# The bonus sums of an RWKV-7 block as narrow float32 strips, with their stores, spreading load and product re-queued

## The chip, the cores and the metric

The kernel runs on one core of one Trainium2 chip. The metric is the device time of one execution in microseconds. Three runs of the kernel before gave 989.61, 990.5 and 990.91; the median is 990.5.

## The reference

One layer of a hybrid trunk for 512 tokens of width 2048, with 16 learned tokens put ahead. One input projection feeds two groups: RWKV-7 time mixing with 16 heads of 64 channels, and a gated short convolution. The part that matters here is the time mixing's bonus term, with r, k and v of shape (tokens, heads, 64):

```python
rh = r.reshape(bsz, L, H, N)
kh = k.reshape(bsz, L, H, N)
vh = v.reshape(bsz, L, H, N)
...
bonus = jnp.sum(rh * kh * r_k[l], axis=-1, keepdims=True) * vh
y_a = (yn + bonus.reshape(bsz, L, D_RWKV)) * jax.nn.silu(g_r)
```

For every token and head the 64 products r k r_k are summed, and the sum scales that head's 64 values of v. Beside it stands the squared length of every k, which normalises the keys (`kk`), the recurrence over tokens, the convolution, the output projection and two norms over the width. Everything is float32; the output is (1, 512, 2048).

## The kernel before

Channels lie on the partitions, tokens run along the rows of a tile, and two heads of 64 channels make one tile of 128: eight head pairs, i = 0 to 7. The projections are products of 128 x 128 weights with 256 or 512 tokens. Weights come from HBM as float32 (tile wr, 128 x 1024), ACT casts each half to a rounded high part and DVE subtracts it from the raw half for a low part (L151, L152, "w"); three products (high with high, low with high, high with low) keep float32 accuracy (L353, L368).

`mains()` is a generator that issues the projections in a fixed order (the lists ps_k, ps_r, ps_v, ps_g, then ps_C, ps_h, ps_B, ps_gc of the convolution) and brings the weights ahead. The other work is laid between them: `fill(ns)` runs the generator for so many nanoseconds of PE work by the planner's own count, `until("v", i)` runs it until that tile is ready, and `later(ns, f)` puts a function, mostly one DMA, into a list that runs when the planner's clock has gone so far; each of these is put behind the newest weight load (`state["dma"]`). So the order on every queue is written by these numbers, and each engine and each DMA queue then takes its instructions in that order. All DMAs of this part are issued by SP.

`prepare(i)` does the time mixing's work for a pair that doesn't depend on the recurrence. It makes the decay and the factors of the chunks (ar, bk), multiplies r by k and r_k in place (L735), forms the Gram products of the chunks on PE (L755, tiles g, and L766 for the 16 learned tokens), and sums the squares of k over each head: `key_norms` (L786) takes the 576 columns of sq in four strips of 144, each a product with a 32-column matrix of ones and zeros at its own 32 columns of PE (L788). For the bonus it splits r into a high and a low part (rk_h by ACT, rk_l by DVE, L665 and L666), multiplies each with a 128 x 128 matrix of ones (two blocks of 64) into zb (L820, L821), which leaves every channel of a head with that head's sum, copies zb over r (L822), multiplies r by v when v is ready (L919) and has it stored to HBM 12500 ns later (rbd, L920). It is loaded again for the last stage (L1227).

Masked Gram blocks go to HBM (sg) and come back as 16 x 16 diagonal blocks (d); the norms take the same way (sn, nd). DVE inverts the blocks step by step into y (L862 to L888). y goes to HBM (sx, L903) and comes back as xT and xo (`load_inverse`, L894 and L895); SP issues these by `later` too, in odd pairs 20500 and 22500 ns on (pair 1: 22500 and 24500). After every odd pair `invert` takes two pairs together: it turns xT into xn by DVE (L948), and PE forms t from it and the Gram blocks (L963). `next_banks` and the pools give the PSUM tiles; "ser" and "misc" are two of their tags.

Other names below: bd, vd, opd, gated and mixd are tensors in HBM to which SP stores; ex is a small product of DVE with which the projection of a shifted tile begins (L403), u, hh and cv are tiles of the convolution, gc and g are gates.

Of the kernel before, what the change touches and what calls it, by code (L numbers as in the profile page):

```python
# [9 lines left out]
F32 = mybir.dt.float32  # L10
F32R = mybir.dt.float32r
I32 = mybir.dt.int32
AF = mybir.ActivationFunctionType
ALU = mybir.AluOpType
# [4 lines left out]
P = 128  # L19
DM = 2048  # L20
KT = DM // P
SEQ = 512
META = 16
L = SEQ + META
CH = 64
NCH = SEQ // CH + 1
LP = NCH * CH
# [5 lines left out]
C_ID, C_GM, C_BM, C_ON = 0, 128, 384, 512  # L33
# [11 lines left out]
    tr=3200, lev=3000, cp=4200, out=1500, begin=19500, p=2900, u=2900, s=4200, mid=1000, last=3700, mix=2600,  # L45
# [44 lines left out]
def hymba_kernel(ctx: ExitStack, tc: tile.TileContext, xt, xtok, front, w_in, w_out, pv, lup, cst, msk, gf, out):  # L90
    nc = tc.nc
    ctx.enter_context(tc.manual_schedule(engines={mybir.EngineType.PE}))
    cp = ctx.enter_context(tc.tile_pool(name="cp", bufs=1))
    dp = ctx.enter_context(tc.tile_pool(name="dp", bufs=2, space=DRAM))
# [3 lines left out]
    cs = cp.tile([P, C_N], F32, name="cs")  # L98
# [74 lines left out]
    rst = xp.tile([P, 4], F32, name="rst")  # L173
    rsx = cq.tile([P, 2 * META], F32, name="rsx")
    la = cq.tile([P, 2, L], F32R, name="la")
    ones = xp.tile([P, P], F32R, name="ones")
    omm = xp.tile([P, 33], F32, name="omm")
    hv = xp.tile([P, 6, 8], F32, name="hv")
    hl = cp.tile([P, 2, 8], F32, name="hl")
# [9 lines left out]
    def tr(name, dt=F32):  # L189
        return cq.tile([P, LP], dt, tag="tr", name=name, bufs=5)  # L190
# [134 lines left out]
            out=hv[:, 4], in0=pvt[:, V_KA : V_KA + 8], scalar1=-0.5, scalar2=1.0, op0=ALU.mult, op1=ALU.add  # L325
        )

    nc.scalar.copy(ones, cs[:, C_BM : C_BM + P])
    FULL = ((0, 272), (272, L))
    TAIL = ((14, 272), (272, L))  # L330
    REAL = ((META, L),)
# [264 lines left out]
    def later(ns, fn):  # L596
        pending.append((clock[0] + ns, fn))
        pending.sort(key=lambda e: e[0])
# [16 lines left out]
    def fill(ns):  # L615
        while ns > 0:
            seen = len(ready)
            t = step()
            if t is None:
                return  # L620
            ns -= t
            if len(ready) > seen:
                ns += FW["evac"]
# [35 lines left out]
        nc.vector.tensor_tensor(out=lo, in0=raw, in1=hi.bitcast(F32), op=ALU.subtract)  # L659
        return hi, lo  # L660

    def split(t, name, n):
        hi = tr(f"{name}_h", F32R)[:, 0:n]
        lo = tr(f"{name}_l", F32R)[:, 0:n]
        nc.scalar.copy(hi, t)  # L665
        nc.vector.tensor_tensor(out=lo, in0=t, in1=hi.bitcast(F32), op=ALU.subtract)  # L666
        return hi, lo

    heads = [(h, slice(64 * h, 64 * h + 64), slice(64 - 64 * h, 128 - 64 * h)) for h in range(2)]

    place = [(i % 2) * 4 + i // 2 for i in range(NPAIR)]
# [11 lines left out]
    def behind(dst, src):  # L683
        with tc.issue_after(state["dma"]):
            nc.sync.dma_start(dst, src)
# [8 lines left out]
    def prepare(i):  # L694
# [43 lines left out]

        sq = tr(f"sq{i}")
        nc.scalar.activation(sq, k, AF.Square, scale=col(V_KK, i))  # L740
        rh, rl = split(r, f"rk{i}", SEQ)
        fill(FW["gram_b" if p else "gram"] + FW["meta"].get(i, 0))

        late = state["step"] > 48
# [16 lines left out]

        def gram_meta():
            z = early or next_banks()
            norms = key_norms(z[0][:, 96 : 96 + NS]) if late else None
            for h, hs, ho in heads:
                nc.tensor.matmul(  # L766
                    z[h][:, 0:META],
                    bk[hs, 0, h : h + 2, :].rearrange("p a s -> p (a s)"),
                    ar[hs, 0, 0, 0:META],
                    start=True, stop=True,  # L770
                )
            norms = norms if late else key_norms(z[0][:, 96 : 96 + NS])
            if p and "levels" in state:
                state["out"] = state.pop("levels").pop(0)(second_level(z))
            with ahead():
                for h in range(2):
                    nc.vector.tensor_tensor(
                        out=gt[:, h, 0, 0:META], in0=z[h][:, 0:META], in1=gmask[:, h, 0:META], op=ALU.mult
                    )
            with ahead():  # L780
                nc.scalar.copy(n2, norms)
            if "out" in state:
                state.pop("out")()
            state["banks"] = z

        def key_norms(z):  # L786
            for j in range(4):
                nc.tensor.matmul(  # L788
                    z[32 * j : 32 * j + 32], cs[:, C_BM + 48 : C_BM + 80], sq[:, j * NS : (j + 1) * NS],
                    start=True, stop=True, tile_position=(0, 32 * j),  # L790
                )
            return z
# [11 lines left out]

        NS = LP // 4
        n2 = tr(f"n2{i}")[:, 0:NS]
        if late:
            gram_meta()
        za = [pz.tile([P, 4, P], F32, tag="tz", name=f"g{i}_1_{h}") for h in range(2)]
# [4 lines left out]
            gram_meta()  # L814
        masked(za, 1, 5)
        masked(zc, 5, 9)
        fill(FW["gram2"] - FW["meta"].get(i, 0))

        zb = pi.tile([P, SEQ], F32, tag="ser", name=f"zb{i}")
        nc.tensor.matmul(zb, ones[:, 0:P], rh, start=True, stop=False)  # L820
        nc.tensor.matmul(zb, ones[:, 0:P], rl, start=False, stop=True)  # L821
        nc.scalar.copy(r, zb)  # L822
        fill(FW["misc"])


        bt = cq.tile([P, 2, NCH - 1, CH], F32, tag="bt", name=f"bt{i}")
        for a in range(2):
# [9 lines left out]
        def blocks(t):  # L837
            return bass.AP(tensor=t.tensor, offset=t.offset, ap=[[BLK, 8 * NCH], [CH, 16], [1, 16]])
# [9 lines left out]
            stash_later(5500 + 1000 * h, i, gt[ho, h], O_KK, 2 * CH, 64 * h, 64)  # L848
            stash_later(7500 + 1000 * h, i, gt[hs, h, :, CH:P], O_BR, CH, 64 * h, 64)
        nd = cq.tile([NB, 16], F32, tag="nd", name=f"nd{i}")  # L850
        behind(d, blocks(sg))
        behind(nd, sn.rearrange("(p s) -> p s", s=16))
        y = cq.tile([NB, 256], F32, tag="y", name=f"y{i}").rearrange("p (s t) -> p s t", t=16)
        nc.gpsimd.memset(y, 0.0)
        nc.vector.tensor_scalar(out=nd, in0=nd, scalar1=1e-24, scalar2=None, op0=ALU.max)
# [60 lines left out]
                    ))  # L916
        until("v", i)
        v = got["v", i]
        nc.vector.tensor_tensor(out=r, in0=r, in1=v[:, CH:LP], op=ALU.mult)  # L919
        later(12500, lambda: nc.sync.dma_start(rbd[i], r))  # L920
        fill(FW["v"])

        vs = cq.tile([P, NCH, CH], F32, tag="vs", name=f"vs{i}")
# [769 lines left out]
```

## Time and profile before

| what | value |
|---|---|
| runs | 990.5 us median (989.61 to 990.91) |
| profiled execution | 989.51 us, its span 987.6 |
| PE | 978.7 us busy, granted clock 0.998 |
| DVE, ACT, POOL | 707.0, 390.4, 127.6 us busy |
| DMA | 176.89 MB, mean 179 GB/s |

A row of the timeline has the start and the length in us, the engine, the line in the kernel, the operation, what it writes and reads, the shapes, and how many instructions the row holds; in brackets stands the idle time ahead and who ended it. PEld is the loading of weights into PE, which runs beside the products. SPq rows are the time in which SP issues a DMA, not the transfer.

### The profile page before, as it was taken

The numbers are of one execution on the slowest core, as the hardware profiler recorded it, in microseconds if no ns is written. First come the engines' busy times: TensorE is split into PE (matmuls) and PEld (weight loads), VectorE is DVE, ScalarE is ACT, GpSimd is POOL, SyncE is SP. The second block draws the span as 40 slices with busy tenths as digits, with TensorE's granted clock in tenths as the row PEclk, the third lists the DMA queues.
The fourth block names the chain that finished last, engine by engine and source line by source line (L and its number), as shares of the span: only waits on it lengthen the run. The fifth ranks groups of instructions, "written<-read, shape, count | busy, mean of one in ns | idle before, by whom it ended". The sixth has DMA issues, their size and how long they took to land.

```text
span 987.6 us, 23392 instructions
## 1 busy us (share of the span) xinstructions
PE 978.7 (99%) x9511; PEld 907.1 (92%) x9511; DVE 707.0 (72%) x1415; ACT 390.4 (40%) x730; POOL 127.6 (13%) x241
## 2 busy tenths in 40 slices
PE   9999999999999999999999999999999999999996
PEld 9999999999998999998999998989889898888885
DVE  6787966578675779653778754355756698997896
ACT  7653432344312434322434323222332326556464
POOL 0120202112010121010111010011211102001001
PEclk9999999999999999999999999999999999999999
DMA  9526586246675374853275856999784798797654
GB/s 323 161 90 159 136 209 168 76 130 146 154 184 166 91 194 116 210 152 112 85 184 123 205 143 188 272 249 270 217 266 118 220 278 221 190 320 182 157 128 170
DMA packets 205532, 176.89 MB, mean 179 GB/s; under 512 B 138545, under 2 KB 168049, under 8 KB 205041
## 3 DMA queue, kind: packets, MB, share of 16 engines
q1 hardware_dynamic: 202976, 166.76, 60.9%
q0 software_dynamic: 2304, 8.39, 5.0%
q8 instruction: 74, 1.21, 0.5%
q14 instruction: 34, 0.27, 0.1%
q10 hardware_dynamic: 144, 0.26, 0.1%
HBM read 139.02 MB, written 36.35 MB: 178 GB/s over the span
## 4 chain that ended last, share of the span: by engine, by line
PE 96%; DVE 2%; issue 1%; DMA 0%; ACT 0%; POOL 0%; POOLq 0%; DVEq 0%; ACTq 0%
PE ps_v L353 9%; PE ps_h L353 9%; PE ps_C L353 9%; PE ps_g L353 9%; PE ps_B L368 9%; PE ps_gc L368 9%; PE ps_k L353 8%; PE ps_r L353 8%; PE M L1384 7%; PE P L1384 3%; PE Q L1384 2%; PE g L755 2%; PE ps_k L368 1%; PE ps_r L368 1%; PE ps_lora L368 1%; PE zy L1141 1%
## 5 line engine op out<-in xcount | busy, mean ns | idle before, releaser
L151 ACT CAST w<-wr 128x512 fp32r<-128x512 f32 x252 | 153.7, 619 | 294.1 <-PE ps_C L353 46.0
L152 DVE TENSOR_TENSOR w<-wr,w 128x512 fp32r<-128x512 f32 x252 | 174.1, 703 | 121.4 <-ACT w L151 120.2
L353 PE MATMUL ps_v<-xh,w 128*128 128x256 f32 (+2 forms) x512 | 84.0, 284 | 0.0
L368 PE MATMUL ps_B<-xh,w 128*128 128x512 f32 x256 | 83.4, 394 | 0.0
L353 PE MATMUL ps_h<-xh,w 128*128 128x256 f32 (+2 forms) x512 | 81.7, 281 | 0.0
L353 PE MATMUL ps_g<-xh,w 128*128 128x256 f32 (+2 forms) x512 | 81.4, 281 | 0.0
L368 PE MATMUL ps_gc<-xh,w 128*128 128x512 f32 x256 | 81.2, 392 | 0.0
L353 PE MATMUL ps_C<-xh,w 128*128 128x256 f32 (+2 forms) x512 | 80.8, 280 | 0.0
L353 PEld LDWEIGHTS ps_v<-xh,w 128*128 128x128 f32 x512 | 73.9, 188 | 0.3
L353 PE MATMUL ps_k<-xh,w 128*128 128x256 f32 (+1 forms) x448 | 73.3, 285 | 0.0
L353 PE MATMUL ps_r<-xh,w 128*128 128x256 f32 (+1 forms) x448 | 72.6, 281 | 0.0
L353 PEld LDWEIGHTS ps_g<-xh,w 128*128 128x128 f32 x512 | 72.0, 189 | 0.6 <-issue 0.2
L353 PEld LDWEIGHTS ps_h<-xh,w 128*128 128x128 f32 x512 | 72.1, 189 | 0.3
L353 PEld LDWEIGHTS ps_C<-xh,w 128*128 128x128 f32 x512 | 71.7, 189 | 0.2
L353 PEld LDWEIGHTS ps_k<-xh,w 128*128 128x128 f32 x448 | 64.7, 188 | 0.4
L353 PEld LDWEIGHTS ps_r<-xh,w 128*128 128x128 f32 x448 | 63.5, 189 | 0.4 <-issue 0.2
L353 PE MATMUL ps_h<-xl,w 128*128 128x256 f32 x256 | 57.3, 281 | 0.0
L368 PEld LDWEIGHTS ps_gc<-xh,w 128*128 128x128 f32 x256 | 47.8, 188 | 10.0
L368 PEld LDWEIGHTS ps_B<-xh,w 128*128 128x128 f32 x256 | 47.9, 188 | 9.6
L353 PE MATMUL ps_C<-xl,w 128*128 128x256 f32 x256 | 56.2, 280 | 0.0
L353 PE MATMUL ps_v<-xl,w 128*128 128x256 f32 x256 | 55.8, 278 | 0.0
L353 PE MATMUL ps_g<-xl,w 128*128 128x256 f32 x256 | 55.4, 278 | 0.0
(383 smaller groups left out, 2141.2 us busy)
## 6 DMA issues: line engine op xcount, KB each, us to landing
wr<-in_w_in_dram SPq DMA_DIRECT2D x126, 512.0 KB
ct<-opd SPq DMA_DIRECT2D x72, 192.0 KB
wo<-in_w_out_dram SPq DMA_DIRECT2D x24, 512.0 KB
x<-in_w_out_dram POOLq DMA_DIRECT2D x16, 512.0 KB, 6.0
opd<-ar SPq DMA_DIRECT2D x8, 576.0 KB
opd<-gt SPq DMA_DIRECT2D x16, 288.0 KB
bd<-bt SPq DMA_DIRECT2D x64, 64.0 KB
bw<-bd SPq DMA_DIRECT2D x16, 256.0 KB
```

The costliest lines, as they stand in the source:

```text
L151: nc.scalar.copy(hi, rq)
L152: low[q] = eng.tensor_tensor(out=lo, in0=rq, in1=hi.bitcast(F32), op=ALU.subtract).ins
L353: nc.tensor.matmul(ps[r][:, 0 : b - a], ww[:, k * P : (k + 1) * P], xx[:, kt, a:b], start=(kt == 0 and n == 0), stop=(kt == KT - 1 and n = ...
L368: nc.tensor.matmul(ps[r], ww[:, w], xx[:, kt, a:b], start=(kt == 0 and n == 0), stop=(kt == KT - 1 and n == 2))
L755: nc.tensor.matmul(z[h][:, c - c0], bk[hs, c, h : h + 2, :].rearrange("p a s -> p (a s)"), ar[hs, c].rearrange("p a s -> p (a s)"), start= ...
L1141: nc.tensor.matmul(zy[e][hs if e else ho, k], t[hs, o : o + CH], x, start=(n == 0), stop=(n == 2))
L1384: nc.tensor.matmul(bank[s], left(prod, jj, m, s), w, start=(jj == 0 and n == 0), stop=(jj == 7 and n == 2))
```

## The change

The high and low part of r, the two products with the matrix of ones, the copy of zb and the matrix itself go. r is float32 when it reaches PE: four strips of 128 of its 512 columns follow the four strips of the key norms, into the other bank of the same pair. ACT copies the 128 x 128 result (nb). Four of its rows hold one head's sums, for 128 tokens each, and four others the other head's; they are stored to HBM (sb) by two small DMAs, one for each head, put behind the load of the diagonal blocks d, and one DMA that reads each head's 512 sums 64 times spreads them over r again (256 KB, 4800 ns on the planner's clock). The load d itself is now issued behind the newest weight load without the helper. r x v is no longer issued when v is ready: it waits on the planner's clock, 18000 ns in odd pairs, 12500 in even ones, 10500 in pair 0, and is put behind the newest low part of a weight. Its store follows 3000 ns later.

```diff
-        rh, rl = split(r, f"rk{i}", SEQ)
...
-            norms = key_norms(z[0][:, 96 : 96 + NS]) if late else None
+            if late:
+                norms, bonus = sums_of(z)
...
             with ahead():
                 nc.scalar.copy(n2, norms)
+                nc.scalar.copy(nb, bonus)
...
-        def key_norms(z):
+        def sums_of(z):
+            return head_sums(z[0][:, 96 : 96 + NS], sq, NS), head_sums(z[1][:, 96 : 96 + P], r, P)
+
+        def head_sums(z, x, n):
             for j in range(4):
                 nc.tensor.matmul(
-                    z[32 * j : 32 * j + 32], cs[:, C_BM + 48 : C_BM + 80], sq[:, j * NS : (j + 1) * NS],
+                    z[32 * j : 32 * j + 32], cs[:, C_BM + 48 : C_BM + 80], x[:, j * n : (j + 1) * n],
                     start=True, stop=True, tile_position=(0, 32 * j),
                 )
...
-        fill(FW["gram2"] - FW["meta"].get(i, 0))
-
-        zb = pi.tile([P, SEQ], F32, tag="ser", name=f"zb{i}")
-        nc.tensor.matmul(zb, ones[:, 0:P], rh, start=True, stop=False)
-        nc.tensor.matmul(zb, ones[:, 0:P], rl, start=False, stop=True)
-        nc.scalar.copy(r, zb)
-        fill(FW["misc"])
-
+        fill(FW["gram2"] - FW["meta"].get(i, 0) + FW["misc"])
...
-        behind(d, blocks(sg))
+        with tc.issue_after(state["dma"]):
+            asked = nc.sync.dma_start(d, blocks(sg)).ins
         behind(nd, sn.rearrange("(p s) -> p s", s=16))
+        sb = dp.tile([2 * SEQ], F32, tag="sb", name=f"sb{i}")
+
+        def put_sums():
+            with tc.issue_after(asked):
+                for h in range(2):
+                    nc.sync.dma_start(sb[h * SEQ : (h + 1) * SEQ].rearrange("(j s) -> j s", s=P), nb[16 * h : P : 32])
+
+        spread = bass.AP(tensor=sb.tensor, offset=sb.offset, ap=[[SEQ, 2], [0, CH], [1, SEQ]])
+        later(1000, put_sums)
+        later(4800, lambda: nc.sync.dma_start(r, spread))
...
-        nc.vector.tensor_tensor(out=r, in0=r, in1=v[:, CH:LP], op=ALU.mult)
-        later(12500, lambda: nc.sync.dma_start(rbd[i], r))
+
+        def bonus_rows():
+            assert ("v", i + 1) not in ready
+            with tc.issue_after(low[max(low)]):
+                nc.vector.tensor_tensor(out=r, in0=r, in1=v[:, CH:LP], op=ALU.mult)
+
+        wait = 18000 if p else 12500 if i else 10500
+        later(wait, bonus_rows)
+        later(wait + 3000, lambda: nc.sync.dma_start(rbd[i], r))
```

The lines behind the change lie 2 to 8 further on or back: the turning of xT is L948 before and L956 now, the loads xT L894 and L895, sx L903 and L904, vd L927 and L935, r x v L919 and L924, rbd L920 and L928, the strips L788 and L784.

What moved is seen at three places. First SP in pair 1, around the inverse's way through HBM (sx, xT and xo belong to it, wr are weights), before:

```order
L159 DMA wr_2149<-in_w_in_dram 128x1024
L927 DMA vd<-vs_1938 32x9x32 x2
L159 DMA wr_2172<-in_w_in_dram 128x1024
L927 DMA vd<-vs_1938 32x9x32
L903 DMA sx_135<-y_1869 72x16x16
L927 DMA vd<-vs_1938 32x9x32
L159 DMA wr_2229<-in_w_in_dram 128x1024
L894 DMA xT_1906<-sx_135 64x9x64
L895 DMA xo_1907<-sx_135 64x4x64
L894 DMA xT_1906<-sx_135 64x9x64
```

Now:

```order
L935 DMA vd<-vs_1937 32x9x32
L928 DMA rbd_79<-r_1309 128x512
L935 DMA vd<-vs_1937 32x9x32
L159 DMA wr_2174<-in_w_in_dram 128x1024
L935 DMA vd<-vs_1937 32x9x32
L904 DMA sx_134<-y_1867 72x16x16
L935 DMA vd<-vs_1937 32x9x32
L159 DMA wr_2231<-in_w_in_dram 128x1024
L895 DMA xT_1904<-sx_134 64x9x64
L896 DMA xo_1905<-sx_134 64x4x64
L895 DMA xT_1904<-sx_134 64x9x64
```

Before, rbd stood further up, ahead of the last four bd stores and of all vd stores; now it stands between two vd stores, ahead of sx and of the loads xT.

Second, DVE in pair 3 where it takes the projection ps_C (ex). tt, y and prod are steps of the inverse, xn is the even pair's. Before:

```order
L152 TENSOR_TENSOR w_3752<-wr_3747,w_3752 128x512
L862 TENSOR_TENSOR tt_3674<-d_3665,nd_3666 72x8
L863 TENSOR_TENSOR y_3669<-tt_3674,nd_3666 72x8
L873 TENSOR_TENSOR prod_3673<-d_3665,y_3669 72x8
L948 STREAM_TRANSPOSE xn_4065<-xT_3080 128x512
L879 TENSOR_REDUCE tt_3674<-prod_3673 72x4
L882 TENSOR_TENSOR prod_3673<-y_3669,tt_3674 72x8
L152 TENSOR_TENSOR w_3781<-wr_3779,w_3781 128x512
L888 TENSOR_REDUCE y_3669<-prod_3673 72x2x2
L403 TENSOR_TENSOR ex<-ps_C_1_3513,rst 128x4
L873 TENSOR_TENSOR prod_3673<-d_3665,y_3669 72x8
```

Now:

```order
L152 TENSOR_TENSOR w_3756<-wr_3751,w_3756 128x512
L401 TENSOR_TENSOR ex<-ps_C_1_3512,rst 128x4
L863 TENSOR_TENSOR tt_3674<-d_3664,nd_3665 72x8
L864 TENSOR_TENSOR y_3669<-tt_3674,nd_3665 72x8
L874 TENSOR_TENSOR prod_3673<-d_3664,y_3669 72x8
L956 STREAM_TRANSPOSE xn_4070<-xT_3079 128x512
L880 TENSOR_REDUCE tt_3674<-prod_3673 72x4
L883 TENSOR_TENSOR prod_3673<-y_3669,tt_3674 72x8
L889 TENSOR_REDUCE y_3669<-prod_3673 72x2x2
L874 TENSOR_TENSOR prod_3673<-d_3664,y_3669 72x8
```

ex has moved ahead of the first steps of the inverse, of xn and of a low part, which follows it now (it stands further down).

Third, the end of the same stretch on DVE, and SP beside it. DVE before, from the second half of hh to the odd pair's xn:

```order
L404 TENSOR_TENSOR hh_4007<-ps_h_1_3885,rs 128x256
L490 SCALAR_TENSOR_TENSOR cv_4014<-u_3870,pvt,cv_4014 128x512 x2
L152 TENSOR_TENSOR w_3878<-wr_3876,w_3878 128x512
L152 TENSOR_TENSOR w_3881<-wr_3876,w_3881 128x512
L152 TENSOR_TENSOR w_3915<-wr_3913,w_3915 128x512
L152 TENSOR_TENSOR w_3918<-wr_3913,w_3918 128x512
L948 STREAM_TRANSPOSE xn_4066<-xT_3706 128x512
```

Now:

```order
L402 TENSOR_TENSOR hh_4013<-ps_h_1_3889,rs 128x256
L488 SCALAR_TENSOR_TENSOR cv_4020<-u_3874,pvt,cv_4020 128x512 x2
L152 TENSOR_TENSOR w_3882<-wr_3880,w_3882 128x512
L152 TENSOR_TENSOR w_3885<-wr_3880,w_3885 128x512
L152 TENSOR_TENSOR w_3919<-wr_3917,w_3919 128x512
L152 TENSOR_TENSOR w_3922<-wr_3917,w_3922 128x512
L924 TENSOR_TENSOR r_3151<-r_3151,v_3326 128x512
L956 STREAM_TRANSPOSE xn_4071<-xT_3706 128x512
```

The product of r and v stands behind four low parts, directly ahead of xn. SP before:

```order
L473 DMA gated_89<-g_3734 128x512
L927 DMA vd<-vs_3729 32x9x32 x4
L903 DMA sx_135<-y_3669 72x16x16
L927 DMA vd<-vs_3729 32x9x32 x2
L894 DMA xT_3706<-sx_135 64x9x64
L895 DMA xo_3707<-sx_135 64x4x64
L894 DMA xT_3706<-sx_135 64x9x64
L895 DMA xo_3707<-sx_135 64x4x64
```

Now:

```order
L935 DMA vd<-vs_3730 32x9x32 x4
L904 DMA sx_134<-y_3669 72x16x16
L928 DMA rbd_81<-r_3151 128x512
L935 DMA vd<-vs_3730 32x9x32 x2
L895 DMA xT_3706<-sx_134 64x9x64
L896 DMA xo_3707<-sx_134 64x4x64
L895 DMA xT_3706<-sx_134 64x9x64
L896 DMA xo_3707<-sx_134 64x4x64
```

The store rbd stands between sx and the loads xT; before, it stood further up, behind the fourth of eight bd stores.

More of the change, by code (lines that the diff above doesn't have):

```diff
@@ L175, in hymba_kernel @@
     la = cq.tile([P, 2, L], F32R, name="la")
-    ones = xp.tile([P, P], F32R, name="ones")
     omm = xp.tile([P, 33], F32, name="omm")
@@ L326, in hymba_kernel @@
         )
-    nc.scalar.copy(ones, cs[:, C_BM : C_BM + P])
     FULL = ((0, 272), (272, L))
@@ L660, in lora_up @@
         return hi, lo
[L662 to L667, printed above, removed]
     heads = [(h, slice(64 * h, 64 * h + 64), slice(64 - 64 * h, 128 - 64 * h)) for h in range(2)]
@@ L771, in gram_meta @@
                 )
-            norms = norms if late else key_norms(z[0][:, 96 : 96 + NS])
+            if not late:
+                norms, bonus = sums_of(z)
             if p and "levels" in state:
@@ L806, in prepare @@
         n2 = tr(f"n2{i}")[:, 0:NS]
+        nb = tr(f"nb{i}")[:, 0:P]
         if late:
```

## The prediction

> **What bounds the kernel now.** I read the page first, then the chain of waits, then the timeline of single engines at the places that the change touches.
>
> ```profile
> span 987.6 us, 23392 instructions
> PE 978.7 (99%) x9511; PEld 907.1 (92%) x9511; DVE 707.0 (72%) x1415; ACT 390.4 (40%) x730; POOL 127.6 (13%) x241
> PE 96%; DVE 2%; issue 1%; DMA 0%; ACT 0%; POOL 0%; POOLq 0%; DVEq 0%; ACTq 0%
> ```
>
> PE is busy for 99% of the span and is 96% of the chain that ended last. So the time moves by two things only: PE work taken out, and PE waits put in. Work on ACT, DVE or a queue counts only where it makes PE wait. The sum is made against the profiled execution, 989.51 us (987.6 of span, 1.9 outside it); the median of the runs is 990.5, so 1.0 is added at the end. A difference of 0.2%, 2.0 us, is about what can be told from none.
>
> **The PE work.** This is PE at head pair 0 (start, length, engine, line, operation; x8 means eight records in the row):
>
> ```profile
> 83.26 0.45 PE L788 MATMUL ps_v<-sq,cs 128*32 128x144 f32 x8
> 83.64 1.23 PE L353 MATMUL ps_r<-xh,w 128*128 128x260 f32 x8
> 87.50 0.40 PE L820 MATMUL zb<-rk_h,ones 128*128 128x512 f32 x1
> 87.97 0.28 PE L353 MATMUL ps_r<-xl,w 128*128 128x256 f32 x1
> ```
>
> The two removed products (L820, and L821 right behind it) take 87.97 - 87.50 = 0.47 us. What comes in are four float32 strips 32 columns of PE wide, over 128 columns, of the form that the key norms have over 144: those are eight records (two passes of four strips), and the next product starts 83.64 - 83.26 = 0.38 later. So the strips run side by side. The new four stand directly behind them, in the same form; scaled by columns they take 0.38 x 128/144 = 0.34 at most, and since part of the 0.38 is the change of form, which is paid once anyhow, at least about half, 0.19. I take 0.27: a gain of 0.20 a pair, 1.6 in eight (between 8 x 0.13 = 1.0 and 8 x 0.28 = 2.2).
>
> [...]
>
> ```profile
> L735 DVE SCALAR_TENSOR_TENSOR r<-r,hv,ta x8: 701/726/747, 75.1 to 528.1; 128x512 f32<-128x512 f32 x8
> L919 DVE TENSOR_TENSOR r<-r,v x8: 680/690/693, 89.0 to 546.7; 128x512 f32<-128x512 f32 x8
> L920 SPq DMA_DIRECT2D rbd<-r x8: 439/480/488, 97.5 to 557.7; - x8
> ```
>
> These are all instructions of a line (least, median, greatest ns; first and last start). The sums need r (L735), done at 75.1 + 0.7 in pair 0, far ahead of the norms at 83.26, so PE doesn't wait there. ACT loses a cast and a copy, DVE a low part, for one 128x128 copy; PE covers both engines (40% and 72% busy), so this counts nothing.
>
> **What the change moves.** The product r x v (L919, 0.69 on DVE) now stands behind late low parts, and the store rbd (L920, 0.48 on SP) waits for it. SP takes its requests in order. In the new order rbd stands ahead of the loads xT of the odd pairs (and in pair 1 ahead of the store sx that they read), and the turning of xT (L948) is what PE needs next for t (L963). Before:
>
> ```profile
> 155.31 0.37 SPq L903 DMA_DIRECT2D sx<-y  x1
> 151.92 0.93 SPq L927 DMA_DIRECT2D vd<-vs  x2
> 162.23 0.61 SPq L894 DMA_DIRECT2D xT<-sx  x1
> 158.04 2.38 DVE L152 TENSOR_TENSOR w<-wr,w 128x512 fp32r<-128x512 f32 x2
> 162.26 0.69 DVE L414 TENSOR_TENSOR gc<-ps_gc,rs 128x512 f32<-128x512 f32 x1 [1.85 <-PE ps_gc L368]
> 169.36 0.70 DVE L948 STREAM_TRANSPOSE xn<-xT 128x512 f32<-128x512 f32 x1
> 169.43 1.36 PE L963 MATMUL t<-xn,gt 64*64 64x32 f32 x64
> ```
>
> Pair 1: the product now stands between the two low parts that end at 158.04 + 2.38 = 160.42 and gc. It is done by 161.1, within DVE's idle 1.85. But SP, which had sent sx at 155.31, now holds at rbd until 161.1: rbd, a vd, a wr and a vd, four issues of about 0.45 (two vd take 0.93), put sx at 162.9. How long a transfer takes is seen at pair 3:
>
> ```profile
> 287.26 0.30 SPq L903 DMA_DIRECT2D sx<-y  x1
> 291.35 0.31 POOL L854 MEMSET y<- 72x256 f32 x1 [1.45 <-DMA sx<-y]
> 291.31 0.60 SPq L894 DMA_DIRECT2D xT<-sx  x1
> 292.64 0.61 SPq L894 DMA_DIRECT2D xT<-sx  x1
> 295.96 0.71 DVE L948 STREAM_TRANSPOSE xn<-xT 128x512 f32<-128x512 f32 x1 [1.32 <-DMA xT<-sx]
> 298.00 1.14 PE L963 MATMUL t<-xn,gt 64*64 64x32 f32 x64
> ```
>
> POOL and SP are both released at 291.3, so sx takes 4.05 from its issue; the second xT, 1.33 behind the first, takes 295.96 - 292.64 = 3.3. Hence in pair 1: 162.9 + 4.05 = 167.0, second xT issued at 168.3, there at 171.6, turned at 172.3. PE wants it half way through t, at about 170.1 (the first half uses the even pair). The wait is 2.2; in pair 5 (below) sx was through in 2.8, and with 2.8 for both transfers 0.4 of the wait is left; with 0.8 more of issue it is 3.0. I take 1.8.
>
> [...]
>
> Pair 3 has two losses in a row. These are DVE, POOL and PE there:
>
> ```profile
> 272.51 0.16 DVE L862 TENSOR_TENSOR tt<-d,nd 72x8 f32<-72x8 f32 x1
> 274.62 0.69 DVE L152 TENSOR_TENSOR w<-wr,w 128x512 fp32r<-128x512 f32 x1 [0.69 <-ACT w L151]
> 275.23 0.15 DVE L888 TENSOR_REDUCE y<-prod 72x4 f32<-72x8 f32 x1
> 276.72 0.16 DVE L403 TENSOR_TENSOR ex<-ps_C,rst 128x4 f32<-128x4 f32 x1 [1.34 <-PE ps_C L353]
> 286.51 0.68 DVE L888 TENSOR_REDUCE y<-prod 72x64 f32<-72x512 f32 x1
> 288.04 0.41 DVE L404 TENSOR_TENSOR hh<-ps_h,rs 128x256 f32<-128x256 f32 x1
> 288.60 1.30 POOL L485 TENSOR_TENSOR u<-u,hh 128x514 f32<-128x514 f32 x1
> 290.69 1.54 DVE L490 SCALAR_TENSOR_TENSOR cv<-u,pvt,cv 128x512 f32<-128x512 f32 x2 [2.24 <-ACT cv L487]
> 292.14 2.49 DVE L152 TENSOR_TENSOR w<-wr,w 128x512 fp32r<-128x512 f32 x4
> 292.93 0.61 PE L368 MATMUL ps_B<-xh,w 128*128 128x512 f32 x2
> ```
>
> DVE waits for PE at ex (276.72). Before, six small steps of the inverse's y, the turning of the even pair's xT and one low part run ahead of it, from 272.51 to 275.38; in the new order they stand behind ex. Without the idle 0.69 they take 2.2, and from ex to the last step of y DVE has no idle time. The two last steps of y now stand between the halves of hh, which lets one half (0.35 of DVE's time) go ahead of them. So y ends at 287.2 + 2.2 + 0.35 = 289.75, and hh, two short instructions later, at 290.3 instead of 288.45. Through u and cv this 1.85 reaches the first low part, which ended at 292.14 + 0.69 = 292.83 and now ends at 294.7; PE uses it in the second product of the row at 292.93, at 293.15. That is a wait of 1.5. (The distances from ex hold whatever PE lost or gained earlier.) The four low parts then end at 296.5, r x v behind them at 297.2, and only then does SP send rbd, 0.48, two vd, 0.93, and the xT loads: the first at 298.6, the second at 300.0, there at 303.3, turned at 304.0. PE would have wanted it at 298.57, half of the 1.14 from 298.00. In all 5.4 of waiting, the 1.5 among them. With 2.8 for xT it is 4.9; if the delay behind ex does not come about, r x v ends at 295.3 and 3.5 is left; with two half microseconds of issue more it is 6.5. I take the middle, 5.0.
>
> Pairs 5 and 7 have the same queue, but more room:
>
> ```profile
> 421.04 0.30 SPq L903 DMA_DIRECT2D sx<-y  x1
> 423.80 0.60 SPq L894 DMA_DIRECT2D xT<-sx  x1
> 426.40 0.75 DVE L432 SCALAR_TENSOR_TENSOR g<-pr_g,omm,sh_g 128x512 f32<-128x512 f32 x1
> 433.80 1.14 PE L963 MATMUL t<-xn,gt 64*64 64x32 f32 x64
> ```
>
> r x v follows g there, at 427.1 to 427.8. There SP sends sx ahead of rbd, and it is through in 423.80 - 421.04 = 2.8, so nothing waits for sx. rbd, vd, wr and vd take 1.8; the xT loads now go out at 429.6 and 430.9, the second is there at 434.2 and turned at 434.9, against a need at 434.4. That is 0.5 in pair 5 and, in the same pattern 147 us later, 0.5 in pair 7; nothing or 1.5 each at the ends. I take 0.8 for both.
>
> In the even pairs SP also holds at rbd, longest in pair 2. Behind it stand weights and vd stores:
>
> ```profile
> 232.69 0.44 SPq L159 DMA_DIRECT2D wr<-in_w_in_dram  x1
> 245.62 0.68 DVE L152 TENSOR_TENSOR w<-wr,w 128x512 fp32r<-128x512 f32 x1
> 259.28 0.28 PE L353 MATMUL ps_g<-xl,w 128*128 128x256 f32 x1
> ```
>
> In pair 2 the product follows the low part at 245.62, so rbd goes at about 247 and the weights sent at 232.69 at 248. With 5 us of transfer (an estimate, one more than sx's 4.05) and 1.3 for cast and low part they are ready at 254.3; by the order of the instructions PE's first use of their low part is the product at 259.28. Five microseconds of cover are left, so this counts nothing. If the cover were gone in all four even pairs by 1 us each, it would be 4.
>
> The sum: -1.6 + 1.8 + 5.0 + 0.8 = +6.0, 995.5 in the profiled execution and **996.5** against the median.
>
> **The rivals.** *Covers hold.* r x v and the transfers behind it come early enough that PE never waits: behind a held SP few requests are open, and sx and xT land faster than in any row above. For it: DVE is busy only 72% and loses a low part a pair; against it: SP's order is fixed, and at pair 3 PE's first use is only 293.15 - 292.83 = 0.32 behind the low part. Then only the PE work counts, -1.6: 988.9, down to 988.3 at the end of its bounds, with no wait in pair 3 as the point that decides; not slower. Chance 0.25.
>
> *Pair 3 alone.* One wait of 1.5 to 3.5 comes and the others are covered: -1.6 + 1.5 to 3.5 = -0.1 to +1.9, 991.5. For it: nowhere else is the room so small; against it: the hold of SP is the same in pair 1. Chance 0.16.
>
> *The strips run one after another.* Eight passes of 128 columns at a quarter of the 0.23 of a product over 512 are 0.47, what was removed: no gain, and 998 with the waits. Against it stands the row of the norms, eight records in 0.38. Chance 0.04. *Weights late too:* the four microseconds of the even pairs on top, 1000.5. For it speaks the long hold of SP, against it the cover of 5. Chance 0.09.
>
> The forecast keeps 0.46, with 993 to 1000 as its own range.
>
> **How the numbers follow.** Slower by over 0.2% (above 992.5) are the forecast, the last two rivals and a little of the second: 0.46 + 0.13 + 0.03 = 0.62. Within 0.2% are most of the second rival and nearly half of the first, 0.13 + 0.11 = 0.24; faster by over 0.2%, under 988.5, is left with 0.14, the end at which the strips cost least and nothing waits. The range from 988.8 to 1000.5 leaves out about two in ten.
>
> **What would show it.** Right: L784 in eight records more in about 0.25 us, a PE wait of 4 to 6 us between 290 and 306 at the products ps_B and t, released by DVE w and xn; xn waiting for the DMA xT at pair 1 and 3; rbd on SP released by DVE r. Wrong: no PE wait of over 1 us in the list of waits, or xT loads that land as early as before; then r x v or the transfers were not where I put them. PE waits at low parts in the even pairs would show the third case.

## The result and the profile after

The changed kernel takes 1016.51 us (median; 1014.11 to 1018.24), beside 990.7 of the kernel before on the same chip: a ratio of 1.0256, interval 1.0241 to 1.0271. It is slower, as forecast, but by 25.8 us and not by 6.0, and 1016.5 lies outside the range. The profiled execution took 1015.02, with a span of 1013.0; against the profiled 989.51 that is 25.5 more.

These lines of the page of the changed kernel are the busy time of the engines, the granted clock in 40 slices and the chain that ended last:

```profile
PE 987.9 (98%) x9559; PEld 915.5 (90%) x9559; DVE 703.9 (69%) x1407; ACT 382.9 (38%) x721; POOL 133.2 (13%) x241
PEclk9999998999899999999999999999999999999999
PE 82%; DVE 9%; DMA 4%; issue 2%; SPq 1%; ACT 1%; POOL 1%; POOLq 0%; DVEq 0%; ACTq 0%
```

Two things are to be seen. PE has fallen from 96% to 82% of the chain: PE waits now. And PE is busy for 9.2 us more than before (978.7), although the change takes PE work out; with that goes a clock that drops to 8 tenths in two slices. The waits of PE, from the list of waits of the same kernel (total, times, longest):

```profile
PE t L971 <- DVE xn L956: 12.9, 4, 4.0
PE ps_C L757 <- DVE pr_g L402: 3.0, 1, 3.0
```

How late PE is can be read at one group, the products z behind t (instructions, durations, first and last start). First the kernel before, then the changed one:

```profile
L976 PE MATMUL z<-xT,ts x128: 219/219/240, 174.1 to 586.4; 64*64 64x32 f32 x128
```

```profile
L984 PE MATMUL z<-xT,ts x128: 219/219/240, 179.7 to 611.7; 64*64 64x32 f32 x128
```

At pair 1 they start 5.6 us late, at pair 7 25.3: all that was lost was lost by then. The same comparison for each of the 6096 projection products, which have the same order in both kernels, gives the steps below. A stop is the distance of two successive starts on PE less what is usual for that product; a step is what PE's lateness grew by from just ahead of the stop until the lateness is level again.

| where | stop of PE | step of its lateness | step less stop |
|---|---|---|---|
| pair 1, t | 3.84 | 6.1 | 2.3 |
| pair 2, Gram product L757 | 3.25 | 6.1 | 2.9 |
| pair 3, ps_B and t | 0.78 + 4.23 | 6.7 | 1.7 |
| pair 5, t | 3.72 | 5.2 | 1.5 |
| pair 7, t | 1.94 | 3.5 | 1.5 |
| sum | 17.8 | 27.6 | 9.9 |

Beside the steps the lateness falls by 0.1 to 0.3 at every pair's strips, 2.0 in all: 27.6 - 2.0 = 25.6. The last column is the surprise. Here is what lies behind it at pair 1, in windows of 1 us (the window, its length, busy time and instructions of PE, PEld, DVE, ACT and POOL, then the granted clock, the share of the DMA engines and GB/s):

```profile
170.00:171.00 1.00, 0.00 (x0) 0.00 (x0) 0.94 (x2) 0.14 (x1) 0.00 (x0) 1.00 0.45 103
172.00:173.00 1.00, 0.00 (x0) 0.00 (x0) 0.71 (x1) 0.00 (x0) 0.00 (x0) 0.52 0.62 102
175.00:176.00 1.00, 1.00 (x6) 1.00 (x5) 0.00 (x0) 0.00 (x0) 0.00 (x0) 0.50 1.02 412
178.00:179.00 1.00, 1.00 (x8) 1.00 (x7) 0.53 (x1) 0.00 (x0) 0.00 (x0) 0.57 0.14 48
```

PE stands still in the first two rows. Towards the end of the stop the granted clock falls to half, and it stays there until 178.9, for 5.9 us after PE has its data at 173.0. Half of these, 2.9, is somewhat more than what PE loses beside the wait (2.3). Behind the other four places the clock is at half for 6.8 us (pair 2) and for 3.4 us each (pairs 3, 5 and 7).

The strips did what they were to do (PE at pair 0, as in the prediction's first row on the PE work):

```profile
83.21 0.45 PE L784 MATMUL ps_v<-sq,cs 128*32 128x144 f32 x8
83.48 0.40 PE L784 MATMUL ps_v<-r,cs 128*32 128x128 f32 x8
83.81 1.23 PE L351 MATMUL ps_r<-xh,w 128*128 128x260 f32 x8
```

From the first strip of the norms to ps_r it is 83.81 - 83.21 = 0.60 where it was 83.64 - 83.26 = 0.38: the four new strips cost 0.22, against 0.47 for what was removed. Eight times 0.25 are the 2.0 above.

**The places.** Pair 1, SP and then DVE:

```profile
160.57 0.34 SPq L928 DMA_DIRECT2D rbd<-r  x1
162.50 0.37 SPq L904 DMA_DIRECT2D sx<-y  x1
167.11 0.62 SPq L895 DMA_DIRECT2D xT<-sx  x1
169.35 0.61 SPq L895 DMA_DIRECT2D xT<-sx  x1
172.28 0.71 DVE L956 STREAM_TRANSPOSE xn<-xT 128x512 f32<-128x512 f32 x1 [1.34 <-DMA xT<-sx]
```

Pair 2, in the order SP, DVE, ACT, PE; this wait was not forecast:

```profile
252.18 0.70 DVE L924 TENSOR_TENSOR r<-r,v 128x512 f32<-128x512 f32 x1
252.90 0.34 SPq L928 DMA_DIRECT2D rbd<-r  x1
253.81 0.45 SPq L159 DMA_DIRECT2D wr<-in_w_in_dram  x1
258.99 1.14 ACT L151 CAST w<-wr 128x512 fp32r<-128x512 f32 x2 [5.89 <-DMA wr<-in_w_in_dram]
259.64 1.29 DVE L152 TENSOR_TENSOR w<-wr,w 128x512 fp32r<-128x512 f32 x2 [4.40 <-ACT w L151]
260.85 0.42 DVE L402 TENSOR_TENSOR pr_g<-ps_g,rs 128x256 f32<-128x256 f32 x1
261.32 0.60 PE L757 MATMUL ps_C<-ar,bk 64*128 64x16 f32 x2 [3.02 <-DVE pr_g L402]
```

The weights behind rbd land 5.2 us after their issue, so the low parts are late. What PE waits for is not these low parts. It is pr_g, the emptying of the bank that the Gram product L757 writes next, and it stands behind the low parts in DVE's order.

Pair 3, SP, DVE and PE:

```profile
308.02 0.34 SPq L928 DMA_DIRECT2D rbd<-r  x1
310.81 0.61 SPq L895 DMA_DIRECT2D xT<-sx  x1
313.86 0.71 DVE L956 STREAM_TRANSPOSE xn<-xT 128x512 f32<-128x512 f32 x1 [5.87 <-DMA xT<-sx]
305.63 0.73 PE L366 MATMUL ps_B<-xh,w 128*128 128x512 f32 x2 [0.62 <-DVE w L152]
314.63 0.67 PE L971 MATMUL t<-xn,gt 64*64 64x32 f32 x32 [4.02 <-DVE xn L956]
```

Pair 5, SP and DVE; PE is 17.4 late by then, so 444.29 stands for 426.9 against the 421.04 of before:

```profile
425.55 5.09 SPq L672 DMA_DIRECT2D opd<-gt  x3
444.29 0.36 SPq L904 DMA_DIRECT2D sx<-y  x1
446.54 0.34 SPq L928 DMA_DIRECT2D rbd<-r  x1
450.15 0.62 SPq L895 DMA_DIRECT2D xT<-sx  x1
452.85 1.29 DVE L152 TENSOR_TENSOR w<-wr,w 128x512 fp32r<-128x512 f32 x2 [5.07 <-ACT w L151]
454.43 0.71 DVE L956 STREAM_TRANSPOSE xn<-xT 128x512 f32<-128x512 f32 x1 [0.28 <-DMA xT<-sx]
```

Here two things are late at once. Ahead of xn DVE stood idle for 5.07 us at two low parts, whose weights SP had sent behind rbd too (447.80); when these were done, xn waited only 0.28 more for xT. In pair 7 it is 4.51 and 0.31.

### The profile page after: what moved, and what is told of

The parts are those of the page before. It is cut to its first block, busy times and chain, and to the rows that moved or that the text cites. A ratio compares the mean times of both kernels' runs of the same rounds, so it can differ in the third digit from the quotient of the medians.

```text
span 1013.0 us, 23511 instructions
## 1 busy us (share of the span) xinstructions
PE 987.9 (98%) x9559; PEld 915.5 (90%) x9559; DVE 703.9 (69%) x1407; ACT 382.9 (38%) x721; POOL 133.2 (13%) x241
## 4 chain that ended last, share of the span: by engine, by line
PE 82%; DVE 9%; DMA 4%; issue 2%; SPq 1%; ACT 1%; POOL 1%; POOLq 0%; DVEq 0%; ACTq 0%
PE ps_B L366 8%; PE ps_v L351 8%; PE ps_C L351 8%; PE ps_g L351 8%; PE ps_gc L366 8%; PE ps_k L351 7%; PE M L1392 7%; PE ps_r L351 7%; PE ps_h L351 5%; PE P L1392 3%; DVE w L152 2%; PE Q L1392 2%; DMA xT<-sx 1%; PE ps_k L366 1%; PE g L745 1%
```

## The experiments

**The store alone moved out of the way.** If SP's hold at rbd is the cause, the store issued behind that pair's loads of the inverse must give most of the time back.

```diff
-        later(wait + 3000, lambda: nc.sync.dma_start(rbd[i], r))
+        def put_rows():
+            with tc.issue_after(state["loaded", i]):
+                nc.sync.dma_start(rbd[i], r)
+
+        later(40000, put_rows)
```

state["loaded", i] is the last load of xo; all else is as in the change.

> The changed kernel with one thing undone: the store rbd of every pair is put behind that pair's xT and xo loads on SP; the product r x v stays where the change put it. Theory A (SP held at rbd makes the loads behind it late): the waits at t in pairs 1, 3, 5 and 7 and at the Gram block in pair 2 go, and the low clock behind each. The price of the strips stays, -2.4, and the late low part of pair 3, about +0.8: 989 us, between 987.5 and 991. Theory B (the late product, the other order on DVE or the added DMAs hold PE up): the store's place does not matter and it stays over 1005.

Measured: 994.38 us (992.19 to 999.91), ratio 1.0059 (1.0036 to 1.0081). 989 was expected; 22 of the 26 us are gone, and with them pair 2's wait. What is left of PE's waits in its profiled execution, 992.19 us:

```profile
PE t L975 <- DVE xn L960: 2.5, 3, 1.1
```

The store's place is the main cause. But the time is not that of the strips alone: in pair 5, SP still sends sx at 427.20 instead of 421.04. A second cause is left.

**The store early in one pair only.** To price single holds, the store was put back to its place in the change for one pair, with the rest as above:

```diff
-        later(40000, put_rows)
+        later(wait + 3000 if i == 1 else 40000, put_rows if i != 1 else lambda: nc.sync.dma_start(rbd[i], r))
```

and the same with 2 for 1.

> As the run before, but pair 1's store stands where the change put it, ahead of sx and xT. Theory A: one PE wait comes back, 3.8 us at t in pair 1, and behind it some 4 us at 0.6 to 0.7 of the clock, so that the time is 6.3 us over the run with all stores behind the loads; 995.3. If the lower clock came from something else than the wait, the difference is 3.8. Theory B: no difference.

> As the first run, but pair 2's store stands where the change put it. Theory A: SP holds some 11 us with weights behind it, DVE holds at their low parts with the taking of ps_g behind them, and PE waits 3.3 us for that bank at the Gram product of the learned tokens; with the clock 6.1 us over the first run, 995.1. If the wait of pair 2 was only a consequence of pair 1's, there is no difference.

Measured: 1001.64 us (ratio 1.0113, 1.0100 to 1.0126) with pair 1's store early, 997.34 (1.0076, 1.0060 to 1.0092) with pair 2's. In the profiled executions PE stops for 4.25 us in pair 1 of the first and is 6.6 later behind it than in the kernel with all stores behind; in the second it stops for 4.21 in pair 2 and is 6.5 later:

```profile
PE ps_C L757 <- DVE pr_g L402: 4.0, 1, 4.0
```

The steps are near those expected of each hold (6.3 and 6.1), though the stops came out longer (4.2 where 3.8 and 3.3 were expected); each costs 2.3 us more than its length. The times expected, 995.3 and 995.1, were missed: the kernel that they start from had come to 994.4 and not to 989, and the kernels' times don't show the step cleanly. The first is 10.2 slower in the profiled execution (1002.35 against 992.19), because pair 3, whose store was not touched, loses 4.7 more there; by the medians it is 7.3. The second is 5.2 and 3.0 slower. The kernel with all stores behind spreads over 7.7 us, so a difference to its median says less than a step within a trace.

**The late product and store without the rest.** The kernel before, with its two products and zb, and only the product r x v and the store of rbd as in the change:

```diff
-        nc.vector.tensor_tensor(out=r, in0=r, in1=v[:, CH:LP], op=ALU.mult)
-        later(12500, lambda: nc.sync.dma_start(rbd[i], r))
+
+        def bonus_rows():
+            assert ("v", i + 1) not in ready
+            with tc.issue_after(low[max(low)]):
+                nc.vector.tensor_tensor(out=r, in0=r, in1=v[:, CH:LP], op=ALU.mult)
+
+        wait = 18000 if p else 12500 if i else 10500
+        later(wait, bonus_rows)
+        later(wait + 3000, lambda: nc.sync.dma_start(rbd[i], r))
```

> The kernel before, with only the last part of the change: the product r x v on the planner's clock behind the newest low part, its store 3000 ns later; the two full products, the copy and the old way of the sums stay. Theory A: SP is held as in the changed kernel; with no gain of the strips 990.7 + 28 = 1018, and at least 1008 where the order on the engines comes out a little otherwise. Theory B's part on added DMAs (the small stores and the spreading load cause the lateness): within 3 us of 990.7.

Measured: 1009.0 us (1004.64 to 1010.07), ratio 1.0179 (1.0161 to 1.0197). Its waits are the change's, smaller in all pairs but the first:

```profile
PE t L970 <- DVE xn L955: 10.0, 4, 3.6
PE ps_C L766 <- DVE pr_g L404: 1.3, 1, 1.3
```

In its pair 5 xn stands on DVE directly behind two late low parts and waits no more for xT:

```profile
448.96 1.29 DVE L152 TENSOR_TENSOR w<-wr,w 128x512 fp32r<-128x512 f32 x2 [5.17 <-ACT w L151]
450.17 0.70 DVE L955 STREAM_TRANSPOSE xn<-xT 128x512 f32<-128x512 f32 x1
```

So the late product and its store cost some 18 us by themselves, and what else the change does costs 7.5 net of the strips' gain. The forecast of this run was 9 us too high: it took the whole loss for the store's.

**What the spreading load costs.** The kernel with the store behind the loads, without the load that spreads the sums (r x v then takes r unsummed, so this part of the computation is left out), and without the two small stores as well:

```diff
-        later(1000, put_sums)
-        later(4800, lambda: nc.sync.dma_start(r, spread))
```

The first kernel leaves out the second of these lines, the second one both.

> As the run with all stores behind the loads, but the load that spreads the sums over r (256 KB, each sum read 64 times) is left out, so r x v takes r without the sum over the head. That run still waited 3.4 us in four places for xT, which went out 2 to 6 us later than before, and came to 994.4. Theory C (the spreading load fills the DMA queue: the four opd stores behind it in pair 5 took 8.4 us of SP, 4.4 before): without it the waits go and only the strips' gain is left, 988.3, at most 989.5. Theory D (the two small stores and the waiting for them, or the product's place on DVE, make xT late): 992 to 994.5.

> As the run without the spreading load, and the two small stores of the sums are left out too (the sums are formed and copied, and go nowhere). Theory C: as the run without the load, within 1 us. Theory D by the stores: 988.3 here and 992 or more there. Theory D by the product's place: 992 or more in both.

Measured: 988.53 us (ratio 0.9980, 0.9971 to 0.9989) without the spreading load, 989.62 (0.9989, 0.9980 to 0.9998) without the small stores too. By the medians the spreading load costs 5.9 us. The small stores cost nothing that shows: the kernel without them was 1.1 slower, at overlapping intervals. Then the load was kept and its shape changed: two loads, one for each head.

```diff
-        later(4800, lambda: nc.sync.dma_start(r, spread))
+        def spread_rows():
+            for h in range(2):
+                one = bass.AP(tensor=sb.tensor, offset=sb.offset + h * SEQ, ap=[[0, CH], [1, SEQ]])
+                nc.sync.dma_start(r[CH * h : CH * h + CH], one)
+
+        later(4800, spread_rows)
```

once in the kernel with the store behind the loads, once in the change as it stands.

> As the kernel whose store goes behind the loads of the inverse (994.38), with the spreading load issued as two loads, one for each head: 64 rows of 512 each, the source's slowest dimension 64 where it was 2; the same 256 KB, the same place. Taking the spreading load out gave 988.53; this asks what of that load costs. Theory H, its shape: the one load keeps few of the DMA engines busy for long, and the requests behind it in SP's queue (the four stores opd in pair 5, 8.45 us against 4.4 without the load) wait for these; two loads with 64 outer rows spread over all engines, opd goes back to 4.4 to 5.5 us, sx of pair 5 to about 422, and the time is 988.5, between 988 and 990. [...] Rival I, the 256 KB themselves or the 64 readings of the same 2 KB fill the engines: opd stays near 8 us and the time at 992 to 999.

> The change as it stands (1016.51) with only the spreading load issued as two loads of 64 rows. Theory H, the load's shape costs in the change too: what is left is the late product and its store, 18.3 in the kernel with these alone (1009.0), less about 2.0 of the strips: 1007, between 1003 and 1010. Rival I, its bytes cost: 1014 to 1018.

Measured: 989.67 us (ratio 0.9989, 0.9980 to 0.9998) in the first, everything computed and still faster than the kernel before. The four stores that SP issues behind the load in pair 5, and the windows of 4 us in which SP is at them; first with the one load:

```profile
407.31 8.45 SPq L672 DMA_DIRECT2D opd<-gt  x4
408.00:412.00 4.00, 4.00 (x37) 4.00 (x36) 1.57 (x6) 0.14 (x1) 0.00 (x0) 1.00 0.77 202
412.00:416.00 4.00, 4.00 (x37) 4.00 (x35) 3.52 (x22) 1.75 (x3) 0.19 (x1) 1.00 0.47 124
```

then with the two loads:

```profile
407.24 4.51 SPq L672 DMA_DIRECT2D opd<-gt  x4
408.00:412.00 4.00, 4.00 (x37) 4.00 (x36) 1.66 (x8) 0.00 (x0) 0.00 (x0) 1.00 0.94 271
```

and without any:

```profile
405.30 4.40 SPq L672 DMA_DIRECT2D opd<-gt  x4
```

With the one load SP needs 8.45 us for the four stores, until 415.8, and meanwhile the DMA engines are busy for 0.77 and then 0.47 of the time: they are not full. With the same bytes in two loads of 64 outer rows it is 4.51, with 0.94. So it is the load's shape that costs, not its 256 KB: 4.7 of the 5.9 us by the medians, and 3.1 of 4.2 by the fastest run of each kernel, since the one with the load in one piece spreads most. The source of the one load has 2 as its outermost dimension (the two heads), that of each of the two loads 64. Whether it is this dimension or the number of loads that counts, and how many engines one transfer keeps busy, is not shown.

In the change itself the same edit gave 1012.99 (ratio 1.0228, 1.0212 to 1.0244): 3.5 us of gain, where 6.5 to 13.5 were expected by the one theory and none to 2.5 by the other. Neither number was met. The late product's stops remain (3.45, 2.71, 4.19, 2.80 and 1.94 in pairs 1, 2, 3, 5 and 7 of its profiled execution), larger from pair 2 on than in the kernel that had only the late product (1.51, 3.40, 2.02, 1.59). Why they are, with a load that no longer holds SP, is not settled; and in that execution 1.9 us were lost near the start, 0.9 of them at a stop of 0.77 at 34.7, where nothing had been changed.

**The price of a stop by itself.** The faster kernel of the next part has almost no waits. In it the turning of xT into xn was repeated, so that PE stops at t in pairs 1 and 5 for a length that is set, while the queues stay as they are:

```diff
-            for q in both:
+            for q in (0,) + (1,) * (1 + {0: 4, 4: 8}.get(first, 0)):
```

with {0: 2, 4: 6} in the second kernel.

> Measures the disputed cost by itself: what a stop of PE costs beside its own length. As the kernel with the odd pairs' spreading load behind the xT loads (988.36), but in pair 1 the turning of xT into xn is done five times and in pair 5 nine times, 0.71 us of DVE each, so that PE stops at t by about 2.85 us more in pair 1 (it waited 0.35 there) and by about 2.9 us in pair 5 (2.7 of room, 8 x 0.71 = 5.7); the queues and the transfers stay as they are. Theory F, the granted clock falls behind a stop and each stop of 3 us costs 1.6 to 2.9 us more than its length: 988.4 + 5.75 + 3.2 to 5.8 = 997.3 to 1000, with windows of granted clock 0.50 behind both. Rival G, a stop costs its length, and what the late transfers cost beside it came from other work that they delayed: 994.1.

> The same with shorter stops: the turning is done three times in pair 1 and seven times in pair 5, for stops at t of about 1.75 us in pair 1 and 1.5 us in pair 5, 2.9 us added in all. Theory F with a cost that grows with the stop (some of the stops of 1.3 to 2.0 us so far cost nothing extra, some 1.6): 991.3 to 994.5, and full clock behind a stop that costs only its length. Rival G, a stop costs its length whatever it is: 991.3.

Measured: 1000.6 us (1000.27 to 1001.14) and 994.66 (993.87 to 995.18), against 988.36 without the added stops. Stop by stop, as in the table above (in pair 1 the 0.35 that it waited anyway is taken off):

| kernel, pair | added stop | step of PE's lateness | step less stop |
|---|---|---|---|
| long, 1 | 2.98 | 5.97 | 3.0 |
| long, 5 | 3.86 | 6.76 | 2.9 |
| short, 1 | 1.49 | 3.08 | 1.6 |
| short, 5 | 2.37 | 3.90 | 1.5 |

That a stop costs its length alone would have given 994.1 and 991.3, and with the stops as long as they came, 6.84 and 3.86 in all, 995.2 and 992.2. It falls. The windows of pair 1 show both prices. With the long stop (PE was back at 172.7):

```profile
172.00:173.00 1.00, 0.30 (x12) 0.30 (x16) 0.65 (x1) 0.00 (x0) 0.00 (x0) 0.75 1.04 293
176.00:177.00 1.00, 1.00 (x6) 1.00 (x6) 0.00 (x0) 0.16 (x1) 0.00 (x0) 0.50 0.14 55
179.00:180.00 1.00, 1.00 (x25) 0.86 (x28) 0.43 (x1) 0.00 (x0) 0.00 (x0) 0.84 0.08 29
```

With the short one (PE was back at 171.5):

```profile
172.00:173.00 1.00, 1.00 (x23) 0.96 (x16) 0.00 (x0) 0.65 (x2) 0.00 (x0) 1.00 0.88 279
173.00:174.00 1.00, 1.00 (x7) 1.00 (x7) 0.00 (x0) 0.00 (x0) 0.00 (x0) 0.60 1.02 301
175.00:176.00 1.00, 1.00 (x7) 1.00 (x6) 0.69 (x1) 0.02 (x1) 0.00 (x0) 0.50 0.18 67
176.00:177.00 1.00, 1.00 (x8) 0.99 (x6) 0.12 (x1) 0.00 (x0) 0.00 (x0) 0.70 0.13 49
```

Half clock for 0.8 + 1 + 1 + 0.6 = 3.4 us loses 1.7; in the long case it lasts from 172.5 to 179.3, 6.8 us, of which PE works through 6.6. The clock falls, in the short case, when PE has been back for 1.7 us: it follows the stop with a delay. In all windows of 1 us read here the clock is 0.50 or 1.00, but for those in which it changes. Half clock lasted either 3.4 us, behind both short stops and in pairs 3, 5 and 7 of the change, or 6.8, behind the long stop of pair 1 and in pairs 1 and 2 of the change.

**A version that keeps the strips.** With the store behind the loads, the odd pairs' spreading load went there too, and r x v behind it; the even pairs keep their load where the change has it:

```diff
-        later(4800, lambda: nc.sync.dma_start(r, spread))
...
-        wait = 18000 if p else 12500 if i else 10500
-        later(wait, bonus_rows)
+        def spread_rows():
+            with tc.issue_after(state["loaded", i]):
+                nc.sync.dma_start(r, spread)
...
-        later(40000, put_rows)
+        if p:
+            later(40000, spread_rows)
+            later(45000, bonus_rows)
+        else:
+            later(4800, lambda: nc.sync.dma_start(r, spread))
+            later(12500 if i else 10500, bonus_rows)
+        later(50000, put_rows)
```

and once more with every spreading load as the two loads shown above.

> Everything computed. As the run with all stores behind the loads, and in the odd pairs the spreading load stands behind the xT and xo loads too, with r x v behind it, after the turning of xT. The even pairs keep the load's place. Theory C: the waits at t, all in odd pairs, go: 988.3 to 989.5, under the kernel before. Theory D: 991 to 994, since the stores keep their place.

> The odd pairs' spreading load behind the xT loads (988.36) and every spreading load issued as two of 64 rows: everything is computed. Theory H, the load's shape keeps SP waiting wherever the load stands, the even pairs included: their four stores opd are sent in the time they took before, the 1.02 of waiting in pair 3 that is left goes, and the time is 987.2, between 986.5 and 988.2. Rival, behind the xT loads the shape no longer matters: 988.4, no different.

Measured: 988.36 us (987.95 to 990.09), ratio 0.9978 (0.9968 to 0.9988), and 989.23 (988.21 to 989.61), ratio 0.9981 (0.9972 to 0.9990). Both compute everything and are faster than both kernels, by 0.2% than the kernel before; the two loads bring nothing more here. That the shape costs wherever the load stands was wrong: behind the xT loads nothing urgent is queued behind it.

## Why the prediction was wrong, step by step

The direction was right, and in pairs 1 and 3 so was the mechanism: r x v late on DVE, SP held at rbd, the loads behind it late, PE waiting at t for xn. In pairs 2, 5 and 7 a second path was missing, and the size was wrong throughout. Term by term, against the profiled execution:

| term | forecast | measured |
|---|---|---|
| strips | -1.6 | -2.0 |
| pair 1 | 1.8 | 3.84 |
| pair 3 | 5.0 | 0.78 + 4.23 = 5.01 |
| pairs 5 and 7 | 0.8 | 3.72 + 1.94 = 5.66 |
| even pairs | 0 | 3.25 |
| half clock behind the stops | not counted | 9.9 |
| sum | +6.0 | +25.7 |

**Right.** The strips run side by side; 2.0 is inside the bounds of 1.0 to 2.2, since four strips cost 0.22 and not 0.27. That part of the 0.38 is paid once shows in the loading of weights, which stands idle for 0.23 us between the strips and ps_r before, and for 0.20 with eight strips. That pair 3 was met is in part luck, since its parts were not: the late low part cost 0.78 and not 1.5, t the more. In pair 1 the queue was met within half a microsecond until sx landed: sx at 162.9 forecast, 162.50 measured; the first xT at 167.0 and 167.11.

**Mis-sized: pair 1.** The second xT was put 1.3 behind the first; it went 2.24 behind, since the issue of xo between them took 1.51 in place of 0.63. xn was then turned at 173.0 and not at 172.3. And PE, 0.6 ahead by the strips, wanted it at 169.2, not at 170.1. Together 3.84 where 2.2 had been worked out. Rounding that down to 1.8 towards a better case was no help. sx itself, for which 4.05 had been taken from pair 3, took 4.6 from its issue to the first xT (162.50 to 167.11).

**Failed: "five microseconds of cover are left, so this counts nothing".** The landing of the weights was well estimated, 5 us against 5.2. But the cover was counted to PE's first use of the low part. DVE takes its work in order too, and behind the two late low parts, from 260.85, stood pr_g, which empties a bank that PE needs earlier than the low part. The prediction asked this question of SP, and not of DVE. The rival "weights late too" had the place, with a chance of 0.09, and 1 us a pair for a price.

**Failed: pairs 5 and 7.** The step moved only the xT loads, by rbd's hold. Between rbd and these loads stand weights, which it counted as an issue and not as something that DVE waits for. Their low parts stand ahead of xn on DVE, and DVE was free of them only 0.28 us before xn began in pair 5. In the kernel with the late product alone, pair 5 waited 2.02 with no wait for xT left, so there the late low parts were what ended last. The loads were late as well: in pair 5 of the change the second xT went out at 432.7 by PE's time, where 430.9 was forecast, and took 4.3 to land, not 3.3. And the queue ahead of rbd no longer stood where it had stood: the spreading load, which the prediction names nowhere as a cost, kept SP at the stores opd, and sx left SP 5.8 late. With the store out of the way that load costs 5.9 us by the medians. How much of the 5.66 is the spreading load's is not shown: with it as two loads pair 5 still stopped for 2.80 and pair 7 for 1.94, and in the kernel without it 2.02 and 1.59 were left.

**Left out: the clock.** The sum took a stop of PE at its length. In the execution of before no PE wait is longer than 1.0 us and the granted clock is 0.998, so the price of a stop could not be read there; but a bound for it was missing too. Nearly two fifths of the loss, 9.9 of 25.5, is PE at half clock after it had its data. No rival and no bound of the range held this term. Only pair 1's and pair 3's forecast stops were of a length, 1.5 us or more, at which most stops here cost 1.5 to 3 us more. With that the forecast would have come to 9 to 12, still under half of the loss.

## What to carry to other kernels

Where PE is busy for 99%, price a stop at its length and, from about 1.5 us on, keep 1.5 to 3 us more in the range: of the 22 such stops at pairs 1 to 7 in these traces 19 cost that and three cost nothing more, and only windows of a run told which. When an instruction waits longer on an in-order engine, list what stands behind it on every engine that is then late in turn, the emptying of PSUM banks first (pr_g cost PE 3.02 us in pair 2), and not only the tile that the late data feed. Look at a DMA's shape before its bytes: 256 KB as one load of 2 x 64 x 512 nearly doubled the time that SP needed for the requests behind it (8.45 us against 4.40 without it), and as two loads of 64 rows it did not (4.51).

## What the runs showed of the hardware that was not expected

The clock's fall depends on more than a stop's length. Stops of 1.49, 1.94 and 2.37 us cost 1.5 to 1.6 beside their length, the 3.84 of pair 1 cost 2.3 and the 4.23 of pair 3 with its 0.78, and the 3.72 of pair 5, only 1.7 and 1.5. Three stops cost nothing more than their length: 2.02 and 1.59 in pairs 5 and 7 of the kernel with only the late product, and 3.45 in pair 1 of the change with the load in two, behind which PE was 3.2 later than ahead of it. Windows of 1 us, one within the stop and one behind it, for the first and then for the last of these, all at full clock:

```profile
450.00:451.00 1.00, 0.07 (x4) 0.07 (x7) 1.00 (x3) 0.00 (x0) 0.00 (x0) 1.00 0.69 178
452.00:453.00 1.00, 1.00 (x10) 0.96 (x9) 0.00 (x0) 0.84 (x3) 0.00 (x0) 1.00 0.81 274
```

```profile
173.00:174.00 1.00, 0.00 (x0) 0.00 (x0) 0.22 (x1) 0.00 (x0) 0.00 (x0) 1.00 1.13 143
176.00:177.00 1.00, 1.00 (x11) 1.00 (x10) 0.00 (x0) 0.06 (x1) 0.00 (x0) 1.00 0.97 385
```

With the stop of 3.84 at the same place in the change came 6.8 us of half clock, so the length alone does not decide. What else does, no run here tells. Half clock may be part of why the kernel with the store behind the loads spread over 7.7 us: its two longest executions, 999.20 and 999.91, had a mean clock of 0.994, its shortest, 992.19, 0.998. It is not why the kernel before spread over 3.0 beside it, whose longest, 992.56, had 0.998.
